# A one-core two-block model: state space layer in plain F32 on VectorE, joined up projections, another place for a weight, and weight splits without GpSimd

## The chip, the cores and the metric

The kernel runs on one core of a Trainium2 chip. The metric is the time of one execution in device microseconds. A core has TensorE (matrix products), VectorE, ScalarE and GpSimd (element by element work), and SyncE, whose queue starts nearly all transfers here. Each engine works through its own instructions in order; engines wait for each other on semaphores. In the profile TensorE is PE (PEld is its weight loading), VectorE DVE, ScalarE ACT, GpSimd POOL and SyncE SP.

## The reference, cut to what matters

The model has 256 tokens, width 1024 and feed-forward width 2816. The first block is a state space layer and stick-breaking attention, each with a feed-forward network behind it whose gate goes through a short convolution; the second has two layers of feed-forward, hybrid mixer, feed-forward. In all there are six networks of the form

```python
def swiglu(x, w13, w2):
    gate, up = jnp.split(x @ w13, 2, axis=-1)
    return (jax.nn.silu(gate) * up) @ w2
```

(two of them with the convolution and other weights). The state space layer is

```python
u = (h @ w_in).reshape(bsz, seq, N_GROUPS, SSM_GROUP)
bu_re = jnp.einsum('blgh,gph->blgp', u, bb_re)
bu_im = jnp.einsum('blgh,gph->blgp', u, bb_im)
_, _, s_re, s_im = lax.associative_scan(combine, (a_seq_re, a_seq_im, bu_re, bu_im), axis=1)
y = jnp.einsum('blgp,ghp->blgh', s_re, c_re) - jnp.einsum('blgp,ghp->blgh', s_im, c_im) + d_skip * u
z = jax.nn.gelu(y.reshape(bsz, seq, D_SSM)) @ w_glu
return z[..., :D_MODEL] * jax.nn.sigmoid(z[..., D_MODEL:])
```

and a mixer ends with `(gate_a * ya + gate_b * yb) @ w_out`, where `ya` and `yb` are two branches behind products of their own.

## The kernel before

**Split products.** Most products are F32 at reduced passes: each operand is split into a high part `h` (a cast) and a low part `l = x - h`, and `mm3` (L179) adds low x high, high x high and high x low in PSUM, three matmuls and three weight loads. `Core.unit` (L158) fetches one weight unit of 128 x 1024 (512 KB) into `raw` (three buffers) on SyncE's queue, casts it on ScalarE into `wh` (L150) and subtracts on VectorE into `wl` (L154). With `share` above zero GpSimd makes that many of the 1024 columns of `wl` in parallel, and VectorE the rest: 512 for units loaded ahead for the next network (`ahead`) and for the mixers' convolutions, 640 for the mixers' z, gate and branch weights and the gate half of `w_glu`, 384 for `w_in`.

**Feed-forward** (`ffn`, L406). The hidden width is 22 columns `m` of 128. Columns 0 and 1 are made ahead of the network by token (`ahead`, `behind`), and the other 20 by `main`: for each of the two halves `c` (gate and up) a chain of eight steps of k, three matmuls of 256 tokens each (`cols_steps`, L199), into one half of a shared PSUM bank. Then `gated`: Silu on ScalarE out of PSUM, the product with the up half on VectorE (L423), and the split into `gh` and `gl`. Seven columns later (`LAG`) the column's down projection follows, twelve matmuls of 512 columns into four accumulating banks; the last six columns are held back and run at the end (`last_rows`). Of eight PSUM banks four accumulate, and at the start two more hold the columns made ahead.

**State space layer** (`ssm`, L501). Z and W hold powers of the decay, built by `step` in growing ranges, Z's on VectorE and W's on GpSimd. `inputs` makes the products with `w_in` (eight units, split as above, against a split input). For each of eight groups kt, `group` makes `gt` from Z and b and `ca` from W and c: a first product on VectorE, a second one (`prod`) on GpSimd, and the addition on VectorE for `gt` and for the first `ca`, on GpSimd for the other seven (`GADD`). Then come the scan and its rotations on VectorE (`t`, `v`, `Sx`), with `turns` (`ea`, `eb`, `er`) four times between. At most three groups are in flight. `weave` fixes TensorE's order by an estimated time, with `inputs` and the first half of the gated output product as filler.

**The output projection of a mixer** (`row_gemm`, L266, with `hold` 5). Units 0 to 2 are used as they come, units 3 to 7 are held, and their products run per output part, over all five each time. Which pool a unit of a stage with `spare` gets is counted by `turn`: every fifth goes to `spare`, the others to the four buffers of `wp`. Held units use the pool `hold` (five buffers, 40,960 bytes a partition) with `hraw` (two raw buffers, 8,192) for their loads; `spare` has 8,192 bytes. The pools lie one on another in the order in which they are opened: `hraw` from 108,768, `hold` from 116,960, `spare` from 157,920 to 166,112. Before, the same bytes belonged to the mixer's own pools, among them `mk2` (123,488 to 150,112), `mk1` (to 164,448) and `keep1` (to 181,856), which holds the gates until the last branch product is gated and split (`gate_b`). Pools are shared out and synchronised by the framework, which also sets the order of instructions on every engine but TensorE.

## Time and profile before

| what | value |
|---|---|
| median of 3 runs | 2254.35 us (2253.45 to 2261.68) |
| the profiled execution | 2259.23 us, of which span 2257.5 us |
| mean granted TensorE clock | 0.976 |
| TensorE busy | 2146.6 us (95%) |
| VectorE busy | 1466.2 us (65%) |
| ScalarE busy | 1102.8 us (49%) |
| GpSimd busy | 510.7 us (23%) |

The profile is that of one execution. Its span is the time between the first and the last instruction. The busy time of an engine is an average over stages; the tables by stretch below are read for a stage. The granted clock is given as a share of full speed.

### The profile page before, as it was taken

The page shows a single profiled execution, that of the slowest core. Times are in us where ns is not written, and L with a number is a line of the kernel's source. Part 1 is how long each engine was busy: PE and PEld are TensorE (multiplying, and loading weights), DVE is VectorE, ACT ScalarE, POOL GpSimd, SP SyncE. Part 2 cuts the span into 40 slices and gives each one's busy share as a digit, 9 for nine tenths or more (in the row PEclk, how much of TensorE's full clock was granted, in tenths as well). Part 3 has the DMA queues.
Part 4 walks back from the last instruction along what each step waited for, and adds up shares of the span by engine and source line. Part 5 has one row for each costly group of instructions (what it writes and reads, how often), then busy time and mean ns, then how long its engine had stood idle before and what let it go on. Part 6 is the DMA issues. An engine that isn't in the chain of part 4 may idle for free.

```text
span 2257.5 us, 40264 instructions
## 1 busy us (share of the span) xinstructions
PE 2146.6 (95%) x15892; PEld 1968.0 (87%) x15892; DVE 1466.2 (65%) x2352; ACT 1102.8 (49%) x1951; POOL 510.7 (23%) x519
## 2 busy tenths in 40 slices
PE   5679999999999999998999899999999899999998
PEld 5568999888999999897889899989989788998997
DVE  8974766676666555689754765565558886466555
ACT  4344554454545544466555444444445656543442
POOL 7542100101000100252534410020015344342000
PEclk8779999999999999999999999999999999999999
DMA  4214576544556556554443655556565454264663
GB/s 153 66 34 149 167 240 188 173 138 140 177 185 197 183 185 187 165 170 145 133 118 121 207 157 186 185 183 197 186 188 157 133 154 122 92 203 154 194 188 121
DMA packets 123486, 362.27 MB, mean 160 GB/s; under 512 B 24732, under 2 KB 38000, under 8 KB 123296
## 3 DMA queue, kind: packets, MB, share of 16 engines
q1 hardware_dynamic: 117696, 350.25, 49.7%
q0 software_dynamic: 5232, 9.37, 1.5%
q8 instruction: 125, 2.05, 0.4%
q14 instruction: 65, 0.53, 0.1%
q10 hardware_dynamic: 368, 0.07, 0.0%
HBM read 355.36 MB, written 5.04 MB: 160 GB/s over the span
## 4 chain that ended last, share of the span: by engine, by line
PE 75%; DVE 10%; DMA 5%; issue 5%; ACT 2%; POOL 1%; ACTq 0%; POOLq 0%; DVEq 0%
PE ps L36 72%; PE ps L40 3%; DVE wl L154 3%; DMA raw<-in_ffn_w_dram 2%; ACT wh L150 2%; DMA raw<-in_w_in_z_dram 1%; DVE xl L154 1%; DMA k<-scratch 1%; DVE keep L1053 1%; DVE k L1053 1%; DVE ea L513 0%; POOL u L1052 0%; DVE keep L1052 0%; DMA raw<-in_w_out_dram 0%; DVE er L709 0%
## 5 line engine op out<-in xcount | busy, mean ns | idle before, releaser
L154 DVE TENSOR_TENSOR wl<-raw,wh 128x1024 fp32r<-128x1024 f32 (+3 forms) x622 | 718.3, 1158 | 543.4 <-ACT wh L150 541.2
L150 ACT CAST wh<-raw 128x1024 fp32r<-128x1024 f32 x622 | 649.4, 1049 | 659.4 <-PE ps L36 344.2
L36 PE MATMUL ps<-xl,wh 128*128 128x256 f32 x3056 | 880.4, 288 | 8.5 <-DVE xl L154 6.2
L36 PE MATMUL ps<-xh,wh 128*128 128x256 f32 x3056 | 866.1, 283 | 0.0
L36 PE MATMUL ps<-xh,wl 128*128 128x256 f32 x3056 | 865.9, 283 | 0.0
L36 PEld LDWEIGHTS ps<-xl,wh 128*128 128x128 f32 x3056 | 587.9, 192 | 32.8 <-issue 19.1
L36 PEld LDWEIGHTS ps<-xh,wh 128*128 128x128 f32 x3056 | 587.2, 192 | 3.9
L36 PEld LDWEIGHTS ps<-xh,wl 128*128 128x128 f32 x3056 | 586.8, 192 | 0.0
L154 POOL TENSOR_TENSOR wl<-raw,wh 128x512 fp32r<-128x512 f32 (+2 forms) x172 | 293.3, 1709 | 1183.9 <-ACT wh L150 1126.7
L36 PE MATMUL ps<-wl,gh 128*128 128x512 f32 x528 | 208.9, 396 | 0.0
L36 PE MATMUL ps<-wh,gl 128*128 128x512 f32 x528 | 208.3, 394 | 0.5 <-DVE gl L154 0.5
L36 PE MATMUL ps<-wh,gh 128*128 128x512 f32 x528 | 208.0, 394 | 0.0
L36 PE MATMUL ps<-wl,xh 128*128 128x256 f32 (+1 forms) x576 | 188.2, 327 | 11.8 <-DVE wl L154 11.8
L36 PE MATMUL ps<-wh,xl 128*128 128x256 f32 (+1 forms) x576 | 183.1, 318 | 0.8 <-DVE xl L154 0.7
L36 PE MATMUL ps<-wh,xh 128*128 128x256 f32 (+1 forms) x576 | 182.4, 317 | 0.0
L36 PEld LDWEIGHTS ps<-wl,xh 128*128 128x128 f32 x576 | 110.7, 192 | 21.4 <-DVE wl L154 12.7
L36 PEld LDWEIGHTS ps<-wh,gl 128*128 128x128 f32 x528 | 99.2, 188 | 24.3 <-DVE gl L154 1.3
L36 PEld LDWEIGHTS ps<-wh,xl 128*128 128x128 f32 x576 | 110.8, 192 | 9.9 <-DVE xl L154 2.7
L36 PEld LDWEIGHTS ps<-wh,xh 128*128 128x128 f32 x576 | 111.0, 193 | 6.5
L36 PEld LDWEIGHTS ps<-wl,gh 128*128 128x128 f32 x528 | 99.7, 189 | 18.8
L36 PEld LDWEIGHTS ps<-wh,gh 128*128 128x128 f32 x528 | 99.2, 188 | 18.5
L150 ACT CAST xh<-ps 128x512 fp32r<-128x512 f32 (+1 forms) x68 | 34.0, 517 | 115.5 <-PE ps L40 113.3
(286 smaller groups left out, 2446.8 us busy)
## 6 DMA issues: line engine op xcount, KB each, us to landing
raw<-in_ffn_w_dram SPq DMA_DIRECT2D x264, 512.0 KB, 4.3
raw<-in_ffn_w_up_dram SPq DMA_DIRECT2D x88, 512.0 KB, 4.1
raw<-in_w_in_qkv_dram SPq DMA_DIRECT2D x48, 512.0 KB, 4.1
raw<-in_ffn_w_down_dram SPq DMA_DIRECT2D x44, 512.0 KB, 3.9
raw<-in_w_in_gate_dram SPq DMA_DIRECT2D x32, 512.0 KB, 3.6
raw<-in_w_branch_dram SPq DMA_DIRECT2D x32, 512.0 KB, 3.6
raw<-in_ssm_w_glu_dram SPq DMA_DIRECT2D x16, 512.0 KB, 3.5
raw<-in_w_in_z_dram SPq DMA_DIRECT2D x16, 512.0 KB, 3.6
```

Source lines behind the costliest of these rows:

```text
L36: self.pe.matmul(out, lhsT=lhsT, rhs=rhs, start=start, stop=stop)
L40: self.pe.transpose(out, in_, ident)
L150: o = [self.nc.scalar.copy(out=h, in_=src).ins]
L154: r = e.tensor_tensor(out=l[..., c], in0=src[..., c], in1=h.bitcast(F32)[..., c], op=ALU.subtract)
L1053: stt = lambda o, a, s, b, op0, op1, e=V: e.scalar_tensor_tensor(out=o, in0=a, scalar=s, in1=b, op0=op0, op1=op1)
```

## The change

(1) In the state space layer the normalised input stays one plain F32 tile, `w_in` is loaded raw and multiplied in plain F32, and all of GpSimd's products and additions go to VectorE. Since the eight `w_in` units no longer pass `unit`, `turn` counts on from another value. (2) In the up projections the high and low parts of the input lie side by side, and a step of k is one matmul of 512 columns (weight high part against both) and one of 256 (weight low part against input high part); each chain takes a PSUM bank of its own, and `fold` adds its two halves (a copy on ScalarE, an addition on VectorE). (3) In the stage of a mixer's output projection `spare` is opened ahead of `hraw` and `hold`, so that it lies from 108,768, `hraw` from 116,960 and `hold` from 125,152 to 166,112. (4) All shares of GpSimd in weight splits go, but for the convolutions'.

```diff
@@ -204,6 +204,28 @@
+    def wide_steps(self, out, w, x):
+        both = out.rearrange("p a b -> p (a b)")
+        for k in range(KD):
+            a = slice(k * P, (k + 1) * P)
+            high = lambda: self.pe.matmul(both, lhsT=w[0][:, a], rhs=x[k][2].rearrange("p a b -> p (a b)"),
+                                          start=k == 0, stop=k == KD - 1)
+            if k < KD - 1:
+                high()
+            self.pe.matmul(out[:, 1], lhsT=w[1][:, a], rhs=x[k][0], start=False, stop=False)
+            if k == KD - 1:
+                high()
+            if k % 3 == 2:
+                yield 1
+    def fold(self, pool, ps):
+        s = pool.tile([P, T], F32, name="sum")
+        self.nc.scalar.copy(out=s, in_=ps[:, 1])
+        self.nc.vector.tensor_tensor(out=s, in0=ps[:, 0], in1=s, op=ALU.add)
+        return s
@@ -228,7 +250,7 @@
             for src in srcs:
-                ws.append([self.unit(src[j], SHARE, stay=True) for j in range(2)])
+                ws.append([self.unit(src[j], stay=True) for j in range(2)])
@@ -314,10 +336,11 @@
-        return tuple(self.hp[i].tile([P, KD, T], F32R, name=f"x{s}") for s in "hl")
+        both = self.hp[i].tile([P, KD, 2, T], F32R, name="xx")
+        return both[:, :, 0], both[:, :, 1], both
     def ktiles(self, x):
-        return [(x[0][:, k, :], x[1][:, k, :]) for k in range(KD)]
+        return [tuple(v[:, k] for v in x) for k in range(KD)]
@@ -381,17 +404,16 @@
-    def silu_gate(self, pool, ps, m):
+    def silu_gate(self, pool, g, m):
         s = pool.tile([P, T], F32, name="s")
-        self.nc.scalar.activation(out=s, in_=ps[:, 0, :], func=AF.Silu)
+        self.nc.scalar.activation(out=s, in_=g, func=AF.Silu)
...
-        def gate(pool, ps, m):
-            g = ps[:, 0, :]
+        def gate(pool, g, m):
@@ -417,10 +439,8 @@
-            def gated(m, ps):
-                s = gate(act, ps, m)
-                p = act.tile([P, T], F32, name="p")
-                nc.vector.tensor_tensor(out=p, in0=s, in1=ps[:, 1, :], op=ALU.mult)
+            def gated(m, s, u, p):
+                nc.vector.tensor_tensor(out=p, in0=s, in1=u, op=ALU.mult)
@@ -440,17 +460,20 @@
                             self.pe.transpose(ps[:, c, t * P:(t + 1) * P], state[c][:, t, m * P:(m + 1) * P], self.ident)
-                    gated(m, ps)
+                    gated(m, gate(act, ps[:, 0, :], m), ps[:, 1, :], act.tile([P, T], F32, name="sum"))
...
                     if m < MF:
-                        ps = self.ps(2, T)
                         for c in range(2):
-                            yield from self.cols_steps(ps[:, c, :], self.unit(up[m - 2, c]), self.ktiles(x))
-                        gated(m, ps)
+                            ps = self.ps(2, T)
+                            yield from self.wide_steps(ps, self.unit(up[m - 2, c]), self.ktiles(x))
+                            if c == 0:
+                                s = gate(act, self.fold(act, ps), m)
+                        u = self.fold(act, ps)
+                        gated(m, s, u, u)
@@ -470,7 +493,6 @@
 LAG = 7
-SHARE = 512
@@ -480,13 +502,8 @@
 HS, HT, GATE, SPACE = 2.7, 5.5, 8, 6.0
-GADD = 1
-WP_ = (1,)
-SH_I = 384
 XO = 1
-SH_Y = 640
 NR = 2
-PT = ()
@@ -601,9 +618,15 @@
                 G.memset(turn[:, 1:], 0.5 * np.pi)
-            hT = c.pair(0)
+            hT = one.tile([P, KD, T], F32, name="hT")
             for t in range(2):
-                c.flip(hT, c.rms(t, c.rms_stat(t), g, c.x[:, t, :]), t)
+                xn = c.rms(t, c.rms_stat(t), g, c.x[:, t, :])
+                for q in range(2):
+                    ps = c.ps(4, P)
+                    for j in range(4):
+                        k = q * 4 + j
+                        PE.transpose(ps[:, j, :], xn[:, k * P:(k + 1) * P], c.ident)
+                    S.copy(out=hT[:, q * 4:q * 4 + 4, t * P:(t + 1) * P], in_=ps)
@@ -666,21 +689,21 @@
-            def step(R, src, dst, n, l, e=V):
+            def step(R, src, dst, n, l):
...
                 ta, tb = (v[:, :, :n] for v in (tmp[:2] if R is Z else tmp[2:]))
-                tt(ta, R[:, :, src], l[:, None, 0:1].to_broadcast(sh_), ALU.mult, e)
-                tt(tb, R[:, ::-1, src], l[:, 1:3, None].to_broadcast(sh_), ALU.mult, e)
-                tt(R[:, :, dst], ta, tb, ALU.add, e)
+                tt(ta, R[:, :, src], l[:, None, 0:1].to_broadcast(sh_), ALU.mult)
+                tt(tb, R[:, ::-1, src], l[:, 1:3, None].to_broadcast(sh_), ALU.mult)
+                tt(R[:, :, dst], ta, tb, ALU.add)
...
             for n, l in ((1, l1), (2, l2), (4, l4)):
-                step(W, slice(0, n), slice(n, 2 * n), n, l, G if WP_[0] else V)
-            step(W, slice(4, 5), slice(8, 9), 1, l4, G if WP_[0] else V)
+                step(W, slice(0, n), slice(n, 2 * n), n, l)
+            step(W, slice(4, 5), slice(8, 9), 1, l4)
@@ -720,13 +743,16 @@
         q1 = c.pool(ctx, "q1", 2)
-        hx = c.ktiles(hT)
         def inputs(kt):
-            w = c.unit(I["ssm_w_in"][kt], SH_I)
+            w = c.raw.tile([P, 1024], F32, name="raw")
+            nc.sync.dma_start(out=w, in_=I["ssm_w_in"][kt])
             pu = c.ps(T)
-            yield from c.cols_steps(pu, w, hx)
+            for k in range(KD):
+                PE.matmul(pu, lhsT=w[:, k * P:(k + 1) * P], rhs=hT[:, k, :], start=k == 0, stop=k == KD - 1)
+                if k % 2:
+                    yield 1
@@ -766,9 +792,8 @@
                 tt(o, f(0), h(x), ALU.mult)
-                tt(p, f(1), h(y), ALU.mult, G)
-                add = (G if R is W and kt >= GADD else V).tensor_tensor(out=o, in0=o, in1=p, op=ALU.add).ins
-                last = last if R is W and kt >= GADD else add
+                tt(p, f(1), h(y), ALU.mult)
+                last = V.tensor_tensor(out=o, in0=o, in1=p, op=ALU.add).ins
@@ -812,7 +837,7 @@
             t1 = q1.tile([P, 8, NC], F32, name="t1")
-            tt(t0, v, Er[:, gs, :], ALU.mult, G if kt in PT else V)
+            tt(t0, v, Er[:, gs, :], ALU.mult)
@@ -821,7 +846,7 @@
             t2, t3 = t0, v
-            tt(t2, sc, Er[:, gs, :], ALU.mult, G if kt in PT else V)
+            tt(t2, sc, Er[:, gs, :], ALU.mult)
...
@@ -1036,10 +1061,7 @@
 LW = 2
-SH_C = (512, 512)
-SH_QA = 0
-SH_G = SH_B = SH_Z = 640
-SH_S = 0
+SH_C = 512
@@ -1122,7 +1144,7 @@
             src = n * NH + m
-            w = c.unit(W("qkv")[src], SH_C[f])
+            w = c.unit(W("qkv")[src], SH_C)
...
@@ -1202,7 +1224,7 @@
             for m in range(KD):
-                w = c.unit(W("gate")[side * KD + m], SH_G)
+                w = c.unit(W("gate")[side * KD + m])
...
@@ -1622,8 +1644,8 @@
             if kind == "mix":
+                c.spare_pool(cn)
                 c.hold_pools(cn, MH, MR)
-                c.spare_pool(cn)
```

## Rows read from the trace of the kernel before

**Rows 1.** Busy time by stretch; columns: stretch, length, then busy us of each engine.

```profile
40.00:105.00 65.00, 38.28 (x262) 31.27 (x262) 64.33 (x49) 24.32 (x46) 44.34 (x18) 0.75 0.30 77
105.00:163.00 58.00, 43.73 (x312) 36.01 (x313) 49.52 (x58) 25.95 (x47) 24.31 (x11) 0.79 0.18 37
163.00:204.00 41.00, 40.99 (x299) 35.26 (x298) 17.58 (x32) 14.41 (x28) 6.46 (x3) 0.94 0.16 32
780.00:840.00 60.00, 60.00 (x449) 57.30 (x448) 32.63 (x40) 27.29 (x39) 0.00 (x0) 1.00 0.62 193
1285.00:1291.00 6.00, 0.02 (x1) 0.02 (x1) 4.44 (x7) 3.34 (x4) 2.08 (x3) 0.71 0.51 137
```

**Rows 2.** VectorE's groups by shape, 0 to 163 us: count, busy us, mean ns.

```profile
L513 DVE TENSOR_TENSOR ca<-W,c_re 128x1152 f32<-128x1152 f32 x7 | 15.6, 2236 | 5.8 <-PE ps L36 5.8
L513 DVE TENSOR_TENSOR gt<-Z,b_re 128x1024 f32<-128x1024 f32 x8 | 13.5, 1702 | 0.0
L513 DVE TENSOR_TENSOR Sx<-t,v 128x248 f32<-128x248 f32 x5 | 10.0, 2009 | 0.0
L770 DVE TENSOR_TENSOR gt<-gt,prod 128x1024 f32<-128x1024 f32 x8 | 9.7, 1212 | 0.1
L709 DVE TENSOR_SCALAR er<-er 128x512 f32<-128x512 f32 x4 | 9.4, 2358 | 0.0
L154 DVE TENSOR_TENSOR wl<-raw,wh 128x640 fp32r<-128x640 f32 x8 | 8.7, 1092 | 0.0
L513 DVE TENSOR_TENSOR eb<-count,turnl 128x512 f32<-128x512 f32 x4 | 8.5, 2115 | 0.0
...
L513 DVE TENSOR_TENSOR ea<-count,turnh 128x512 f32<-128x512 f32 x4 | 6.3, 1585 | 0.2 <-ACT Er L717 0.2
L521 DVE TENSOR_SCALAR sm<-sm 128x64 f32<-128x64 f32 x11 | 5.6, 641 | 0.0
L513 DVE TENSOR_TENSOR ea<-ea,er 128x512 f32<-128x512 f32 x4 | 5.0, 1258 | 0.1
...
L513 DVE TENSOR_TENSOR ea<-ea,eb 128x512 f32<-128x512 f32 x4 | 2.7, 680 | 0.0
```

**Rows 3.** GpSimd's groups by shape, whole span.

```profile
L513 POOL TENSOR_TENSOR prod<-W,c_im 128x1152 f32<-128x1152 f32 x8 | 20.6, 2572 | 7.2 <-DVE gt L770 7.0
L770 POOL TENSOR_TENSOR ca<-ca,prod 128x1152 f32<-128x1152 f32 x7 | 19.9, 2848 | 27.0 <-DVE ca L513 27.0
```

**Rows 4.** Timeline of TensorE in a steady feed-forward stretch: start, us.

```profile
862.32 0.28 PE L36 MATMUL ps<-xl,wh 128*128 128x256 f32 x1
...
868.07 0.40 PE L36 MATMUL ps<-wl,gh 128*128 128x512 f32 x1
...
870.87 0.28 PE L36 MATMUL ps<-xl,wh 128*128 128x256 f32 x1
```

**Rows 5.** Timeline of TensorE around 1020 us: four plain F32 records.

```profile
1020.06 1.02 PE L36 MATMUL ps<-keep 128*128 128x256 f32 x4
1020.92 0.38 PE L40 MATMUL ps<-ident,k 128*128 128x128 f32 x2
```

**Rows 6.** VectorE's groups by shape, whole span.

```profile
L154 DVE TENSOR_TENSOR wl<-raw,wh 128x1024 fp32r<-128x1024 f32 x450 | 551.6, 1229 | 457.4 <-ACT wh L150 456.4
L154 DVE TENSOR_TENSOR wl<-raw,wh 128x384 fp32r<-128x384 f32 x80 | 79.8, 997 | 45.6 <-ACT wh L150 45.4
...
L423 DVE TENSOR_TENSOR p<-s,ps 128x256 f32<-128x256 f32 x132 | 54.7, 414 | 1.8 <-ACT s L386 0.9 <-ACT s L401 0.8
```

**Rows 7.** Chain of waits, 1283 to 1300 us: start, us, what.

```profile
1281.59 3.73 DMA raw<-in_ffn_w_dram
...
1287.11 1.50 DVE xl L154
...
1288.62 1.05 ACT wh L150
...
1290.98 9.13 PE ps L36 x32
```

More of the change, by code (lines that the diff above doesn't have):

```diff
@@ L934, in keys @@
         def keys(m):
-            w = c.unit(I["kv_w_k"][m], SH_S)
+            w = c.unit(I["kv_w_k"][m])
             pk = c.ps(T)
@@ L949, in query @@
         def query(m):
-            w = c.unit(I["attn_w_q"][m], SH_S)
+            w = c.unit(I["attn_w_q"][m])
             pq = c.ps(T)
@@ L1164, in plain @@
         def plain(src, dst, scale):
-            w = c.unit(src, SH_QA)
+            w = c.unit(src)
             p = c.ps(T)
@@ L1174, in qkv_a @@
             p = c.ps(2, T)
-            yield from c.toks256_steps(p, W("va")[0], hT, SH_QA)
+            yield from c.toks256_steps(p, W("va")[0], hT)
             ka["v"] = keep2(2, T)
@@ L1189, in z_gate @@
             p = c.ps(2, T)
-            yield from c.toks256_steps(p, W("z")[n], hT, SH_Z)
+            yield from c.toks256_steps(p, W("z")[n], hT)
             z_done(n, p)
@@ L1212, in branch @@
             for m in range(KD):
-                w = c.unit(I["w_branch_2"][side, i, m], SH_B)
+                w = c.unit(I["w_branch_2"][side, i, m])
                 p = c.ps(T)
```

2 lines of the change are left out of this document (1 added, 1 removed).

## The prediction

> **What bounds the kernel now.** I read the table of busy time by stretch first, because the share over the whole span (TensorE 95%) hides that one stage is bound by another engine. In the steady feed-forward stretch TensorE is busy for 60.00 of 60 us at granted clock 1.00, and VectorE for about half of it; in the state space layer from 40 to 105 us it is VectorE that is busy for 64.33 of 65 us, with TensorE at 38.28 us and granted clock 0.75, and GpSimd at 44.34 us [rows 1]. From 105 to 163 us neither is full (VectorE 49.52, TensorE 43.73 of 58), and from 163 to 204 us TensorE is, 40.99 of 41 [rows 1]. So VectorE's time counts up to about 163 us, and from there on TensorE's pace, except at a few places. Then I read VectorE's forms up to 163 us against the same shape elsewhere [rows 2], GpSimd's forms [rows 3], TensorE's pace from start to start (ends are modelled, so I use distances of starts) [rows 4, 5], the weight splits [rows 6], and the chain of waits where TensorE stands still before an output projection [rows 7].
>
> **State space layer.** The change does three things here. (a) GpSimd's arithmetic goes to VectorE. What VectorE pays: second products 8 x 1.212 (1024 wide) and 8 x 1.364 (1152 wide, 1.212 x 9/8), seven additions of 1152 at 1.364, together 30.2 us; and twelve operations on W, for which no free row of the shape stands here: between 0.25 us each (a 64-column operation can't be dearer than the 0.414 of 256 columns) and 0.68 (512 wide), 3 to 8 us; most are 256 wide or less, so I take 5. Sum +35.2 us [rows 2, 6]. What it gets back: the same forms are stretched now, in the stretch in which GpSimd works. Against the free price of their width: gt 8 x (1.702 - 1.212) = 3.9; ca 7 x (2.236 - 1.364) = 6.1; Sx 5 x (2.009 - 0.414) = 8.0; er 4 x (2.358 - 0.680) = 6.7; eb 4 x (2.115 - 0.680) = 5.7; ea 4 x (1.585 - 0.680) = 3.6 and 4 x (1.258 - 0.680) = 2.3; the 64-column operations at least 11 x (0.641 - 0.414) = 2.5. Sum -38.8 [rows 2, 6]. GpSimd's own pieces last as long as these stretches (2.57 and 2.85 us) [rows 3]. (b) w_in is no longer split, nor the layer's input: 8 x 1.092 = 8.7 and four halves of 0.68 = 2.7 go, -11.4 [rows 2]. Net of (a) and (b): 35.2 - 38.8 - 11.4 = -15.0 us of VectorE. In addition a product of 1152 that took 2.57 us on GpSimd, and its addition that took 2.85, take 1.36 each [rows 3]; a group's next step waits for them, 2.7 us a group. With eight groups, three of them in flight together, I count a quarter of that, 5 us. That gives -20. Lower bound of the gain: 3, if VectorE's stretched time was waiting that comes back as waiting for TensorE between 105 and 163 us, where it has room of 8.5 us already. Upper bound: 38, all of the stretched time, if what I priced as moved falls into gaps.
>
> The Trainium skill (SBUF — State Buffer, "SBUF: two separate sides") says that VectorE and GpSimd share one pair of ports, held for a whole instruction, and that the loser is blocked until it ends. Taken at its word all of the 38.8 us goes with GpSimd's work, as I count; the rows agree in size, a stretched Sx of 2.01 beside GpSimd's pieces of 2 to 3 us.
>
> (c) The eight input products become plain F32. Two records of one such product with 256 columns stand 0.86 us per four records, 0.43 per product [rows 5], where the three split ones are 0.36 [rows 4]: 64 x (0.43 - 0.36) = +4.5 us of TensorE work. Up to 105 us TensorE is idle for more than 26 us [rows 1], so I cost it at nothing; if that cover is gone it costs the 4.5. The Trainium skill (FP8 and Floating Point Precision, "TensorE Precision Notes") gives true FP32 four passes, against three reduced ones here; by that alone it would be four thirds of 0.36, 0.48, and +7.7 us; the row is lower and decides. Without the splits the first product also starts earlier; that lies within the range.
>
> **Up projections.** 6 networks x 20 columns m x 2 x 8 = 1920 steps of k. A step is three matmuls of 256 columns now: 48 of them lie between 862.32 and 868.07, 0.120 each, 0.360 a step [rows 4]. It becomes one of 512 columns and one of 256: twelve of 512 take 868.07 to 870.87, 0.233 each [rows 4], so 0.353. The 512 columns were measured with weight rows as moving operand, and next to each other; nothing here shows the two sizes in turn. Bounds: 0.347 (the saved weight load takes another 6 ns with it) to 0.362 (the change of size costs what is saved). I take 0.354, 6 ns x 1920 = -11 us; range -25 to +4. Added is the fold: per chain a copy of 256 columns on ScalarE and an addition of 256 on VectorE, 0.41 us each (the price of p, which also reads PSUM) [rows 6]. Per column m of 8.5 us that is 0.82 on each; VectorE is busy for 32.63 and ScalarE for 27.29 of 60 us [rows 1], so it fits: nothing, for as long as it runs beside the next chain. A column uses two PSUM banks instead of one, and four are free beside the accumulators, so two columns, 17 us, are in flight. At the start of a network two of the four still hold the state: +1 us over the six networks, between 0 and 6.
>
> **Weight place.** In the two output projections after the mixers TensorE stops; in the first it is busy for 0.02 of the 6.00 us from 1285 to 1291 [rows 1]. The second mixer has the same code. The chain runs: a feed-forward weight lands (1281.59 + 3.73), is cast and split, the last gate split ends (1287.11 + 1.50), then the cast and the split of the third output weight, then TensorE [rows 7]. That weight lies in `spare`, which overlaps the mixer's pool `keep1`, and its cast waits for the last user of that pool though the tile itself does not touch it. With the order of the pools turned, `spare` lies at the lowest address, where the mixer is done early; `hold` (five units) now reaches 1,664 bytes into `keep1`. So I expect these 6 us to go and the five held units to wait for the same split instead: late next is the fifth. With R the end of that split: two are cast and split at R + 2.3 and R + 3.5, as their raw tiles are free early; `hraw` has two buffers, so the next two come a load (3.7), a cast (1.05) and a split (1.23) later, at about R + 8.5 and R + 9.7, and the fifth at R + 14.6. The last loop needs it after 4 x 0.69 us and has 3 x 3.4 + 0.7 us of products left, so the end is R + 25.6. Before, the end was 1310.0. Behind these loads on SP's queue stand the next network's four first weights; they are needed only at that end. R is the open number: 1288.6 as now gives +4.2, 1286 (the split next to GpSimd takes 1.50, free 0.41, and its wl before it is no longer halved) +1.6, and 1281, right behind the last branch product, -3.4. I take +2 for each mixer, +4. If the wait is only for the tiles that overlap, four units are ready early, and the gain is 6 to 8 each, -14. Range -16 to +14.
>
> **GpSimd's split shares.** 80 splits go from 0.997 on VectorE, for 384 of 1024 columns, to 1.229 for all of them [rows 6], and 36 of half width I price the same: 116 x 0.232 = 27 us more of VectorE work, and GpSimd's part of each goes. VectorE has room there (32.63 of 60 us in the steady stretch [rows 1]), so nothing, but at the ends of networks the splits of the weights loaded ahead stand before the normalisation on VectorE: +0.5 us at some six of them, +2 net of the lock that goes; range -3 to +4.
>
> **Sum.** -20 - 11 + 1 + 4 + 2 = -24 us. The profiled execution took 2259.23 us, 4.9 above the median of the runs (2254.35), so 2235 in its own terms, and **2230 us** in terms of the median.
>
> **Rivals.** *The state space layer is TensorE's after all.* For it: from 163 us on TensorE is full, and at 105 to 163 us it has 43.73 of 58 at clock 0.79 [rows 1]. Then VectorE's 15 us come back as waiting, the 4.5 us of F32 count, and only 8 net are gained there: 2242 us. *The pair of sizes is no faster.* Then the up projections give 0 to +4 instead of -11: 2242 us. *More comes than I count.* The output projections lose their stop without a new one (-14 in place of +4) or the whole stretched time goes (-32 in place of -20): 2200 to 2216 us. *Slower: the fold stops the chain.* ScalarE works in order. If its queue holds the fold of a chain ahead of the cast of the next chain's weight, the cast waits for the chain's end, and TensorE for 0.41 (copy) + 0.4 (Silu) + 1.05 (cast) + 1.23 (split) = 3.1 us. Between the two chains of a column no product of the down projection lies, so nothing covers it; 120 such places make up to 370 us, and from 8 of them on the gain is gone; at one in six the time is 2292 us. Against it: the steady stretch has no gap in TensorE [rows 1] though Silu stands at the same place, so casts run at least one unit ahead.
>
> **Chances.** Forecast 0.54 (its own range 2214 to 2246); layer bound by TensorE 0.13; no faster pair 0.10; more than counted 0.14; slower by the fold 0.09. A measurement of this kernel tells 0.5%, 11.3 us, from no change. Faster by more than that, below 2243: nearly all of the forecast, half of the next two, all of the fourth, 0.77. Within: 0.14. Slower: 0.09. Range: 2202 to 2250; the slower rival and the far end of the fourth lie outside.
>
> **What would show it.** Right: VectorE's Sx, er and eb near their free price, the end of the layer near 183 us instead of 203; in the steady stretch a step near 0.354 and no gap in TensorE; at the output projections no stop after the second unit but one before the last held unit, with casts of held units right behind the last gate split. Wrong: TensorE waiting for ScalarE or VectorE within up chains, a step of 0.36 or more, or a VectorE that stays full up to 160 us.

## The result, and the profile after

The changed kernel takes 2224.90 us (median of 4 runs, 2223.28 to 2227.32) against 2256.64 us of the kernel before beside it: a ratio of 0.9858, 95% interval 0.9835 to 0.9882, or 31.7 us less. The profiled execution has a span of 2221.5 us, 36.0 less than that of before; of the difference to 31.7, some 4 us is the spread of single executions (2259.23 us is 2.6 above the median of before, 2223.28 is 1.6 below that of after).

The starts of a few products of TensorE, read from the timelines of the two profiled executions, split the 36 us by stage:

| TensorE has come to | before, us | after, us | gained in the stage |
|---|---|---|---|
| first down product of network 1 (state space layer, gated output) | 290.13 | 266.96 | 23.2 |
| last down product of network 3 (networks 1 to 3, attention) | 944.47 | 919.21 | 2.1 |
| last branch product, first mixer | 1279.00 | 1248.54 | 5.2 |
| first product behind its output projection | 1310.02 | 1282.12 | -2.6 |
| last down product of network 5 | 1692.66 | 1660.66 | 4.1 |
| last branch product, second mixer | 2027.81 | 1991.56 | 4.3 |
| first product behind its output projection | 2059.43 | 2025.63 | -2.5 |
| last down product of network 6 | 2248.13 | 2212.18 | 2.1 |

One profile is not sharper than this: four profiles of kernels with the same code up to the first row have it between 261.6 and 267.0 us, and the two with the code of before at 285.88 and 290.13, so differences of a few us in that stage are not read from it: its gain lies between 19 and 29 us.

Busy time by stretch of the changed kernel; columns as in [rows 1]: the stretch, its length, busy us (and instructions) of TensorE, its weight loading, VectorE, ScalarE and GpSimd, then the granted clock, the DMA share and GB/s.

```profile
40.00:105.00 65.00, 56.21 (x379) 47.52 (x377) 54.92 (x77) 35.75 (x60) 0.00 (x0) 0.87 0.38 96
105.00:163.00 58.00, 50.12 (x340) 41.95 (x341) 36.24 (x59) 27.19 (x50) 0.00 (x0) 0.85 0.22 39
...
780.00:840.00 60.00, 60.00 (x317) 51.09 (x316) 37.33 (x51) 31.96 (x50) 0.00 (x0) 1.00 0.60 186
```

Against [rows 1]: from 40 to 105 us GpSimd is at 0, VectorE at 54.92 us instead of 64.33, and TensorE is busy for 56.21 us instead of 38.28, at clock 0.87 instead of 0.75. In the steady stretch TensorE is still full, with 317 matmuls instead of 449. VectorE's groups by shape, 0 to 163 us (count, busy us, mean ns):

```profile
L530 DVE TENSOR_TENSOR prod<-W,c_im 128x1152 f32<-128x1152 f32 x8 | 10.8, 1349 | 0.0
...
L530 DVE TENSOR_TENSOR ca<-W,c_re 128x1152 f32<-128x1152 f32 x8 | 10.7, 1348 | 6.0 <-PE ps L36 6.0
...
L530 DVE TENSOR_TENSOR Sx<-t,v 128x248 f32<-128x248 f32 x7 | 2.9, 408 | 0.0
...
L530 DVE TENSOR_TENSOR eb<-count,turnl 128x512 f32<-128x512 f32 x4 | 2.7, 682 | 0.0
```

The stretched forms of [rows 2] are at the free price at which I had set them: Sx 0.408 instead of 2.009, eb 0.682 instead of 2.115, ca 1.348 instead of 2.236; the product that took 2.57 us on GpSimd [rows 3] takes 1.35. Only er, a scalar operation, came lower than set: 0.416, not 0.680. The layer's last output product starts at 182.2 us instead of 198.2. TensorE in the steady stretch, timeline (start, us):

```profile
780.73 0.27 PE L36 MATMUL ps<-xx,wl 128*128 128x256 f32 x1
...
781.08 0.28 PE L36 MATMUL ps<-xx,wl 128*128 128x256 f32 x1
...
782.81 0.28 PE L36 MATMUL ps<-xx,wl 128*128 128x256 f32 x1
```

The smaller matmul is shown; six steps from 780.73 to 782.81 make 0.347 each, and the mean over 755 to 905 us is 0.350 (0.117 and 0.233). Before, a step was 0.360 [rows 4], and 0.357 on the mean. Last, the chain of waits in the first mixer's output projection (start, us, what); [rows 7] answers to it.

```profile
1252.02 0.35 DVE xx L154
...
1252.39 1.06 ACT wh L150
...
1253.47 1.24 DVE wl L154
1254.72 5.78 DMA raw<-in_w_out_dram
...
1260.53 1.05 ACT wh L150
...
1261.60 1.24 DVE wl L154
1262.86 3.45 DMA raw<-in_w_out_dram
...
1266.33 1.05 ACT wh L150
1267.40 1.24 DVE wl L154
...
1268.69 10.63 PE ps L36 x39
```

The last gate split ends at 1252.37, and at 1252.39 ScalarE casts held units. The third waits for a load (5.78 us) behind the split of the first, the last for another (3.45), and TensorE goes on at 1268.69. The stop ahead of unit 2 in [rows 7] is gone; two others have come, of 4.8 us behind 1258.06 and of 3.5 us behind 1265.19.

### The profile page after: what moved, and what is told of

It reads as the page before. It is cut to its first block, busy times and chain, and to the rows that moved or that the text cites. A ratio compares the mean times of both kernels' runs of the same rounds, so it can differ in the third digit from the quotient of the medians.

```text
span 2221.5 us, 36550 instructions
## 1 busy us (share of the span) xinstructions
PE 2135.0 (96%) x13908; PEld 1867.4 (84%) x13908; DVE 1537.0 (69%) x2615; ACT 1182.5 (53%) x2187; POOL 226.9 (10%) x360
## 4 chain that ended last, share of the span: by engine, by line
PE 74%; DVE 8%; DMA 7%; issue 4%; ACT 3%; POOL 1%; POOLq 0%; SPq 0%; DVEq 0%; ACTq 0%
PE ps L36 71%; PE ps L40 3%; DVE wl L154 3%; ACT wh L150 2%; DMA raw<-in_w_out_dram 2%; DMA raw<-in_ffn_w_dram 1%; DMA raw<-in_ffn_w_down_dram 1%; DMA raw<-in_w_in_z_dram 1%; DMA raw<-in_ssm_w_glu_dram 1%; DVE keep L1075 1%; DMA k<-scratch 1%; DVE prod L530 1%; POOL k L1074 0%; DVE k L1075 0%; DMA raw<-in_kv_w_v_dram 0%
## 5 line engine op out<-in xcount | busy, mean ns | idle before, releaser
L36 PE MATMUL ps<-xx,wh 128*128 128x256 f32 (+1 forms) x4064 | 1077.4, 340 | 4.6 <-DVE xx L154 2.6
L154 DVE TENSOR_TENSOR wl<-raw,wh 128x1024 fp32r<-128x1024 f32 (+1 forms) x614 | 738.1, 1204 | 332.5 <-ACT wh L150 322.7
L36 PE MATMUL ps<-xx,wl 128*128 128x256 f32 x2992 | 803.4, 282 | 0.6 <-DVE wl L154 0.6
L36 PEld LDWEIGHTS ps<-xx,wh 128*128 128x128 f32 x4064 | 686.4, 191 | 91.9 <-issue 18.9
L36 PEld LDWEIGHTS ps<-xx,wl 128*128 128x128 f32 x2992 | 568.4, 190 | 22.0 <-DVE wl L154 0.8
L36 PE MATMUL ps<-wh,xx 128*128 128x256 f32 (+1 forms) x1152 | 258.3, 318 | 0.8 <-DVE xx L154 0.7
L36 PE MATMUL ps<-wl,xx 128*128 128x256 f32 (+1 forms) x576 | 189.7, 329 | 19.3 <-DVE wl L154 18.7
L36 PEld LDWEIGHTS ps<-wh,xx 128*128 128x128 f32 x1152 | 193.5, 193 | 16.5 <-DVE xx L154 3.0
L226 DVE TENSOR_TENSOR sum<-ps,sum 128x256 f32<-128x256 f32 x240 | 101.2, 423 | 112.1 <-ACT sum L225 112.1
L36 PEld LDWEIGHTS ps<-wl,xx 128*128 128x128 f32 x576 | 111.0, 193 | 31.9 <-DVE wl L154 22.6
```

What stands on the lines that cost most here:

```text
L36: self.pe.matmul(out, lhsT=lhsT, rhs=rhs, start=start, stop=stop)
L154: r = e.tensor_tensor(out=l[..., c], in0=src[..., c], in1=h.bitcast(F32)[..., c], op=ALU.subtract)
L226: self.nc.vector.tensor_tensor(out=s, in0=ps[:, 0], in1=s, op=ALU.add)
```

## The experiments

Each kernel is timed beside the kernel before; the ratio to it stands with its 95% interval (0.9858, 0.9835 to 0.9882, for the changed one). Differences are those of the medians (2224.90 us for the changed kernel); taken through the ratios they come out within 1.8 us of these. Where the intervals of two kernels overlap, their difference is not clear of noise, and the text says so.

**GpSimd's arithmetic back in the state space layer.** Theory: VectorE's operations stand while GpSimd works. Rival: the gain came from the input product.

```diff
-                step(W, slice(0, n), slice(n, 2 * n), n, l)
+                step(W, slice(0, n), slice(n, 2 * n), n, l, G)
...
-                tt(p, f(1), h(y), ALU.mult)
-                last = V.tensor_tensor(out=o, in0=o, in1=p, op=ALU.add).ins
+                tt(p, f(1), h(y), ALU.mult, G)
+                add = (G if R is W and kt >= 1 else V).tensor_tensor(out=o, in0=o, in1=p, op=ALU.add).ins
+                last = last if R is W and kt >= 1 else add
```

> The changed kernel with GpSimd's arithmetic of the state space layer back on GpSimd (the steps of W, the second products, seven additions); the plain F32 input product stays. Theory (VectorE's operations stand still while GpSimd works, and VectorE sets the pace up to 163 us): Sx, er, eb and ca are stretched again (Sx near 2 us instead of 0.41), and the layer with its gated output ends 12 to 22 us later than in the changed kernel, 2237 to 2247 us. Rival (most of the 23 us came from the input products without splits): less than 8 us slower, under 2233 us.

Measured: 2259.44 us, ratio 1.0015 (1.0004 to 1.0027): 34.5 us slower than the changed kernel, and no faster than the kernel before. Theory and rival both set it too low; the rival falls. Its profile, busy time by stretch, then VectorE's forms to 163 us, then timelines of GpSimd and VectorE (start, us, in brackets the idle time before and who ended it):

```profile
40.00:105.00 65.00, 43.16 (x242) 35.12 (x242) 50.26 (x50) 23.32 (x43) 24.95 (x10) 0.71 0.25 62
105.00:163.00 58.00, 38.20 (x254) 32.60 (x253) 40.34 (x41) 22.55 (x41) 19.62 (x8) 0.76 0.26 71
```

```profile
L530 DVE TENSOR_TENSOR ca<-W,c_re 128x1152 f32<-128x1152 f32 x6 | 14.3, 2402 | 9.7 <-PE ps L36 9.7
...
L530 DVE TENSOR_TENSOR eb<-count,turnl 128x512 f32<-128x512 f32 x4 | 8.5, 2114 | 0.0
...
L530 DVE TENSOR_TENSOR Sx<-t,v 128x248 f32<-128x248 f32 x4 | 3.5, 869 | 0.1
```

```profile
83.35 2.37 POOL L530 TENSOR_TENSOR prod<-W,c_im 128x1152 f32<-128x1152 f32 x1 [4.17 <-DVE gt L796]
102.57 3.53 POOL L796 TENSOR_TENSOR ca<-ca,prod 128x1152 f32<-128x1152 f32 x1 [16.86 <-DVE ca L530]
106.18 2.89 POOL L530 TENSOR_TENSOR prod<-Z,b_im 128x1024 f32<-128x1024 f32 x1
```

```profile
92.39 0.43 DVE L530 TENSOR_TENSOR t<-t,Er 128x256 f32<-128x256 f32 x1
101.13 1.36 DVE L530 TENSOR_TENSOR ca<-W,c_re 128x1152 f32<-128x1152 f32 x1 [8.32 <-PE ps L36]
```

The forms are stretched again (eb 2.11, ca 2.40, Sx 0.87). But VectorE is busy for only 50.26 of 65 us here, less than in the changed kernel, and the first down product starts 34.6 us later all the same, at 301.51 us. So VectorE's busy time is not the whole price. GpSimd finishes a product at 85.7 and then stands for 16.86 us until 102.57, since its next piece, an addition, needs `ca` from VectorE, and VectorE makes that `ca` only at 101.13, 8.32 us idle, when TensorE has let its buffer go. The product of the next group stands behind the addition in GpSimd's queue and starts at 106.18. The three engines wait for each other in turn, and with one engine fewer in the round each turn is shorter. That is read from these rows; no run tests it by itself.

The 34.5 us are the price in this kernel, with the plain F32 input. In the kernel before, with the same arithmetic on GpSimd and split inputs, the first down product starts 11 to 16 us earlier than here (285.88 and 290.13 us in two profiles). The two kernels differ there in the plain input, the shares, the joined chains and the counter of turns; which of them costs this beside GpSimd was not separated. With split inputs the same stage goes from 286 to 290 us with GpSimd's arithmetic to 257 to 263 without it (three profiles), 23 to 33 us, the shares in it taken out too.

**Split inputs instead of plain F32.** The input and `w_in` are split again, on ScalarE and VectorE alone; the counter of turns moves back with it.

```diff
-            w = c.raw.tile([P, 1024], F32, name="raw")
-            nc.sync.dma_start(out=w, in_=I["ssm_w_in"][kt])
+            w = c.unit(I["ssm_w_in"][kt])
             pu = c.ps(T)
-            for k in range(KD):
-                PE.matmul(pu, lhsT=w[:, k * P:(k + 1) * P], rhs=hT[:, k, :], start=k == 0, stop=k == KD - 1)
-                if k % 2:
-                    yield 1
+            yield from c.cols_steps(pu, w, hx)
```

> The changed kernel with the layer's input and w_in split into high and low parts again, on VectorE and ScalarE alone (no GpSimd), three matmuls a step; GpSimd's arithmetic stays on VectorE, and the counter of turns moves back by eight units, so that in the output projections unit 2 holds spare as before the change. Theory: VectorE gets 8 x 1.23 + 4 x 0.68 = 12.5 us more ahead of its work, TensorE 4.5 us less; up to 60 us VectorE is the later one, so 4 to 12 us slower, 2229 to 2237 us. Rival (plain F32 costs TensorE what the splits cost VectorE): within 3 us of 2225.

Measured: 2222.74 us, 0.9845 (0.9826 to 0.9864): 2.2 us faster, which is not clear of noise: as the rival has it, not 4 to 12 slower. But two things differ, so the counter was moved alone.

**The counter of turns alone.**

```diff
-        self.early, self.norm, self.spare, self.turn = None, [], None, 0
+        self.early, self.norm, self.spare, self.turn = None, [], None, 3
```

> The changed kernel with nothing changed but the counter of turns, which starts at 3, so that the same units go to spare as before the change (in the output projections of the mixers unit 2, in the state space layer's gated output those of before); the input product stays plain F32. The kernel with split inputs (2222.7 us) began the first down projection of the first network 10 us earlier than the changed kernel and lost 6 of them again further on, and both the plain product and the counter differ in it. If the plain F32 product is what costs the 10 us, this kernel keeps that cost and takes over the later losses: 2225 to 2232 us, first down projection near 267 us. If the counter is what costs them (a stop of 3.8 us for a weight of the gated output stands at 203 us in the changed kernel and not there), it begins near 257 us and the time is 2218 to 2223 us.

Measured: 2229.35 us, 0.9878 (0.9861 to 0.9895): 4.5 us slower than the changed kernel, with intervals that overlap, and the first down product at 265.1 us. So the first expectation holds, and the counter is not what cost the 10 us. That the counter costs the 4.5 us is not shown. The two output projections do last 36.3 and 35.9 us instead of 33.6 and 34.1, 4.5 us together; but in four kernels with the counter and the pools of the changed one (chains undone, GpSimd's arithmetic back, shares back, fold doubled) they last 34.2 to 36.9 us too. There the load behind the first held split varies: 7.63 us with the chains undone and 7.10 with the fold doubled, in the first mixer, against 5.78. And the profile with the moved counter has a first mixer that is 5.7 us longer and three networks and an attention that are 4.2 us shorter than the changed kernel's.

With the counter the same, splitting the inputs gives 2222.74 against 2229.35: the plain F32 product costs some 6.6 us. Two later pairs with four held units, told below, give 8.1 (2204.12 against 2196.04, the counter moved) and 3.8 us (against 2200.35, the counter the same), so 4 to 8 us; by the intervals each of the three is known to some 5 to 7 us only, but they have one sign. The plain products among TensorE's groups to 204 us, in the kernel with counter 3:

```profile
L36 PE MATMUL ps<-hT,raw 128*128 128x256 f32 x128 | 31.6, 398 | 0.0
```

Their records take 31.6 us. Over all profiles with the arithmetic on VectorE the layer's last output product starts at 177 to 182 us with plain inputs (eight kernels) and at 166 to 171 with split ones (three), 11 us earlier on the mean. Of this lead 7 us are lost again: from there to the first down product it takes 83 to 85 us with plain inputs and 91 with split ones. The rest is of the size of the 4 to 8 us. No mechanism is shown for either part.

**The joined chains of the up projections undone.**

```diff
-                        for c in range(2):
-                            ps = self.ps(2, T)
-                            yield from self.wide_steps(ps, self.unit(up[m - 2, c]), self.ktiles(x))
...
+                        ps = self.ps(2, T)
+                        for c in range(2):
+                            yield from self.cols_steps(ps[:, c, :], self.unit(up[m - 2, c]), self.ktiles(x))
+                        gated(m, gate(act, ps[:, 0, :], m), ps[:, 1, :], act.tile([P, T], F32, name="sum"))
```

> The changed kernel with the up projections' chains as before: three matmuls of 256 columns a step of k into half of a shared bank, no fold (the input stays side by side in one tile). Theory: the joined step saves TensorE 6.7 ns (0.350 instead of 0.357 in the steady stretch of the two profiles) in 1920 steps, 13 us, and the fold is hidden: 9 to 14 us slower than the changed kernel, 2234 to 2239 us. Rival (the fold or the second PSUM bank costs something at the ends of networks that the steady stretch does not show): less than 6 us slower, under 2231 us.

Measured: 2233.44 us, 0.9897 (0.9881 to 0.9913), 8.5 us slower; between the two expectations and next to the theory's, since the two intervals leave it open by about 6 us. From the first product behind the second output projection to the last down product, the last network takes 188.71 us against 186.55: 2.16 us, which would make 13 for six. Of the 11.5 us between the two profiles 4.7 lie in the output projections (36.6 and 35.8 us instead of 33.6 and 34.1), which the edit does not touch. So the step is worth 8 to 13 us, by an estimate from these two numbers.

**The fold doubled.** The copy twice, and one more operation on VectorE, in each of 240 chains.

```diff
         self.nc.scalar.copy(out=s, in_=ps[:, 1])
+        self.nc.scalar.copy(out=s, in_=ps[:, 1])
         self.nc.vector.tensor_tensor(out=s, in0=ps[:, 0], in1=s, op=ALU.add)
+        self.nc.vector.tensor_tensor(out=s, in0=s, in1=s, op=ALU.max)
```

> The changed kernel with the fold's work doubled: the copy on ScalarE is made twice and VectorE makes one more operation of 256 columns behind the addition, in each of the 240 chains (0.37 us and 0.41 us more). Theory (both lie beside TensorE's products, with room for them): no more than 2 us slower, 2223 to 2227 us. Rival (fold on the path, now and then or always): a tenth of 240 x 0.8 is 19 us; 5 us or more slower, 2230 us or more.

Measured: 2227.67 us, 0.9870 (0.9850 to 0.9890): 2.8 us, neither expectation, and not to be told from none by the intervals. The busy time in the steady stretch:

```profile
780.00:840.00 60.00, 60.00 (x318) 51.09 (x317) 42.78 (x66) 35.96 (x65) 0.00 (x0) 1.00 0.57 186
```

VectorE rises from 37.33 to 42.78 us and ScalarE from 31.96 to 35.96, and TensorE stays full. The last network, with 40 of the 240 doubled folds, takes 139.09 us from its first to its last down product, 139.08 in the changed kernel. So of 187 us of added work none shows there, and in the total no more than the noise lets through, some 10 us.

**The order of the two pools, in both kernels.** First the changed kernel with the old order, then the kernel before with the new order and nothing else.

```diff
                 c.spare_pool(cn)
                 c.hold_pools(cn, MH, MR)
-                c.spare_pool(cn)
```

(the second; the first is its reverse.)

> The changed kernel (2224.9 us) with the two pools of a mixer's output projection opened in the old order again; all else as changed. In the changed kernel the stage from the last branch product to the first product of the next network lasts 33.6 us in the first mixer and 34.1 in the second (31.0 and 31.6 before the change). My theory, that a pool which overlaps the mixer's gate pool waits as a whole for the last gate split, says: now only spare waits, and since the counter of turns has moved it holds unit 0 instead of unit 2, so TensorE stops once, for some 6 us, ahead of unit 0, and then runs through eight units without a stop: 6 + 8 x 2.8 + 1.5 = 30 us, 3 to 4 us less than changed for each mixer, 2217 to 2219 us in all. Rival (the new place is what helps, and what costs 2.5 us a mixer lies elsewhere): the stage gets longer than 34 us, 2227 us or more.

Measured: 2230.80 us, 0.9880 (0.9862 to 0.9897), 5.9 us slower, with intervals that overlap: against the theory's number, and in the rival's range. The stage lasts 33.8 and 35.5 us, 0.2 and 1.4 more than changed; the other 7 us of the profile lie in the second mixer ahead of that stage and were not pursued (on VectorE the framework ordered some weight splits otherwise there). The stop ahead of unit 0 is there, as the theory says, but lasts 9 us, not 6:

```profile
1251.29 1.23 DVE wl L154
...
1253.32 0.44 DVE xx L154
1253.78 1.05 ACT wh L150
...
1256.14 5.88 PE ps L36 x17
```

The gate split ends only at 1253.76, later than I took it, behind a weight of the next network. From the first product there is no further stop.

> The kernel before, with nothing changed but the order of these two pools. The whole-pool wait says: the stop ahead of unit 2 goes, and stops ahead of the last held units come, the last of them ready at R + 14.6 to 16.3 with R about 1288; the stage lasts 33 to 36 us instead of 31: 2 to 5 us more for each mixer, 2260 to 2267 us. Rival (the place alone removes the stop): 24 to 26 us a stage, 2242 us.

Measured: 2268.59 us, 1.0052 (1.0039 to 1.0066), 12 us slower than the kernel before, a little over the upper end of the theory's range; the rival falls. The stage lasts 37.5 and 36.9 us instead of 31.0 and 31.6. The chain of waits shows the same sequence as in the changed kernel: gate split, cast, split, a load of 5.83 us, and another of 3.60 before TensorE goes on.

```profile
1283.07 1.45 DVE xl L154
...
1284.54 1.06 ACT wh L150
...
1286.88 5.83 DMA raw<-in_w_out_dram
...
1295.06 3.60 DMA raw<-in_w_out_dram
...
1301.04 2.07 PE ps L36 x4
```

So by itself the new place costs 12 us in the kernel before; in the changed kernel, with the counter moved, it costs nothing that the stage would show. With the old order the counter decides which unit waits: the stop is ahead of unit 2 and 6.6 us long in the kernel before, and ahead of unit 0 and 9 us long in the changed one.

**Four held units instead of five.** Then the pool of held units ends below the gate pool.

```diff
-MH, MR = 5, 2
+MH, MR = 4, 2
```

> The changed kernel with four held units instead of five in the mixers' output projections (MH 4), so that the hold pool ends at 157,920 and no longer reaches into the gate pool; unit 3 goes through the ordinary buffers. By the theory of the whole-pool wait the stops of 4.4 and 2.9 us ahead of the last held units go, and the stage lasts about 8 x 2.8 + 2 = 24 to 27 us: 7 to 10 us less for each mixer, 2205 to 2211 us. Rival (the held units wait for their loads and the two raw buffers, not for the gate pool): the stage stays above 31 us, 2220 us or more.

Measured: 2204.12 us, 0.9765 (0.9750 to 0.9780), 20.8 us faster than the changed kernel. The stages last 22.9 and 22.8 us. Busy time of the two stages, of this kernel and then of the changed one:

```profile
1244.10:1267.00 22.90, 22.90 (x108) 18.83 (x106) 16.38 (x25) 6.56 (x8) 1.69 (x2) 1.00 0.62 207
1981.50:2004.20 22.70, 22.70 (x106) 18.71 (x105) 14.51 (x21) 6.19 (x7) 1.69 (x2) 1.00 0.56 186
```

```profile
1248.60:1282.10 33.50, 26.20 (x106) 20.40 (x106) 19.72 (x26) 10.07 (x12) 1.69 (x2) 0.85 0.50 187
1991.60:2025.60 34.00, 26.37 (x107) 20.49 (x106) 19.45 (x25) 9.85 (x12) 1.69 (x2) 0.90 0.55 183
```

TensorE is full, 22.90 of 22.90 us at clock 1.00, against 26.20 of 33.50 at 0.85. The two raw buffers are still two. And the eight loads of the output weight are all issued by 1241.03 us, before the last gate split ends at 1250.00; in the changed kernel the last three are issued from 1254.72 on, behind that split (1252.37). So the loads were late because the held casts waited for the gate pool. (One held unit fewer would also shorten the row of loads behind such a wait; here there is no wait left for it to follow.)

**GpSimd's shares back** in the units loaded ahead and in the mixers' z, gate and branch weights.

```diff
-                w = c.unit(W("gate")[side * KD + m])
+                w = c.unit(W("gate")[side * KD + m], 640)
...
-                ws.append([self.unit(src[j], stay=True) for j in range(2)])
+                ws.append([self.unit(src[j], 512, stay=True) for j in range(2)])
```

> The changed kernel with GpSimd's shares back in the units loaded ahead (512 columns) and in the mixers' z, gate and branch weights (640); the state space layer, up projections and pools as changed. My prediction had +2 us for taking them out, so by it this kernel is about 2 us faster, 2223. Against it stands the trace: between the last down product of a network and the last branch products of the mixer behind it the changed kernel is 4.8 us shorter in the first mixer and 3.8 in the second; if that is the shares, this kernel is 6 to 10 us slower, 2231 to 2235 us.

Measured: 2236.21 us, 0.9912 (0.9893 to 0.9930), 11.3 us slower. From the last down product before a mixer to the first product of its last branch it takes 315.8 and 314.1 us, 307.7 and 309.2 in the changed kernel; the output projections take 36.2 and 36.4 instead of 33.6 and 34.1. The profiled execution is the slowest of six (2243.33 us), so by stage the loss looks larger than it is. Two stretches of the first mixer, of this kernel and of the changed one:

```profile
976.00:1076.00 100.00, 88.70 (x627) 78.20 (x627) 83.71 (x184) 59.12 (x123) 40.50 (x55) 0.95 0.46 143
1076.00:1180.00 104.00, 102.03 (x986) 92.45 (x985) 68.39 (x196) 58.96 (x187) 43.59 (x62) 0.98 0.36 109
```

```profile
975.00:1075.00 100.00, 91.44 (x661) 81.42 (x660) 84.45 (x193) 62.30 (x133) 38.88 (x54) 0.97 0.48 148
1075.00:1170.00 95.00, 95.00 (x946) 85.56 (x944) 60.63 (x187) 55.27 (x175) 19.11 (x46) 1.00 0.38 113
```

The first stretch of 100 us holds 627 matmuls with the shares and 661 without, at clock 0.95 and 0.97; the second has 986 in 104 us against 946 in 95. Over both, with 1613 and 1607 matmuls, VectorE is busy for 152.1 us with the shares and for 145.1 without, in 204 and 195 us, though with them it has fewer columns to split. Over the whole first mixer, up to its last branch, it is even, in 315.8 and 307.7 us:

```profile
920.90:1236.70 315.80, 302.52 (x2563) 276.46 (x2562) 220.61 (x503) 177.66 (x425) 140.59 (x162) 0.98 0.43 136
```

```profile
919.20:1226.90 307.70, 299.12 (x2563) 273.68 (x2562) 221.35 (x503) 177.49 (x425) 88.12 (x131) 0.99 0.45 139
```

The splits of weights take VectorE 68.1 us of it with the shares and 77.4 without, and everything else 152.5 against 144.0: what it saves in columns it loses in longer operations beside GpSimd (a form of 128 x 256, `keep` from `k`, sixteen times, takes 0.759 us on the mean instead of 0.689). TensorE has the same 2563 matmuls and is busy 3.4 us longer, at clock 0.98 instead of 0.99, and idle 4.7 us longer. Which wait makes the mixer longer was not found, nor which of the two sets of weights does it.

**The last share out too** (the convolutions'), on top of four held units: `SH_C` 0 for 512.

> Four held units, and the last share of GpSimd, that in the 48 convolution weights, taken out too; else as the changed kernel (2204.1 us with four held units alone). VectorE gets 48 x 0.29 = 14 us more and GpSimd 77 us less. If the shares cost what they cost elsewhere in the mixers (4 to 5 us a mixer for some 40 units), 2194 to 2200 us. If VectorE, which is busier in the stretch of the convolutions, becomes the late one there, 2206 to 2216 us.

Measured: 2215.64 us, 0.9821 (0.9803 to 0.9838): 11.5 us slower than with four held units alone. The first expectation falls, the second holds. The first mixer takes 320.2 us up to its last branch against 307.2, so there the share pays. Which stage of it loses shows in its busy time against that of the kernel with four held units alone, from the start of the mixer:

```profile
914.90:974.00 59.10, 57.66 (x447) 52.99 (x446) 45.38 (x75) 34.93 (x57) 5.81 (x11) 1.00 0.52 158
974.00:1074.00 100.00, 88.11 (x606) 77.69 (x605) 77.33 (x175) 55.71 (x117) 23.91 (x44) 0.93 0.45 132
```

```profile
914.80:974.00 59.20, 59.18 (x461) 54.73 (x460) 49.38 (x82) 35.80 (x59) 29.42 (x26) 1.00 0.48 151
974.00:1074.00 100.00, 91.79 (x667) 81.83 (x665) 84.55 (x195) 61.83 (x135) 36.51 (x53) 0.97 0.48 152
```

TensorE falls from 59.18 to 57.66 and from 91.79 to 88.11 us, at clock 0.93 instead of 0.97 in the second. Its waits for VectorE in the mixer come to 10.4 us against 2.2 with four held units alone; the two longest (us in total, times, longest us):

```profile
PE ps L36 <- DVE keep L1075: 4.0, 1, 4.0
PE ps L36 <- DVE wl L154: 2.6, 1, 2.6
```

So VectorE is the late one there.

**Four held units and split inputs together.**

> Four held units (2204.1 us alone) and split inputs (2222.7 alone, 2.2 under the changed kernel) together. With four held units the output projections of the mixers have no stop whichever unit goes to spare, so what the split inputs lost there does not come back: 10 us less than four held units alone, 2193 to 2200 us. If the gain of the split inputs is only a shift between stages, 2201 to 2206 us.

Measured: 2196.04 us, 0.9735 (0.9716 to 0.9753): 60 us under the kernel before and 29 under the changed one, the fastest of all; the first expectation holds. With the counter as in the changed kernel besides (`turn` from 2):

> Four held units and split inputs (2196.0 us) with the counter of turns started at 2, so that the units that go to spare are those of the changed kernel. In the changed kernel moving the counter back cost 4.5 us, as much as the two output projections got longer (36.3 and 35.9 us instead of 33.6 and 34.1). If that is the only way in which the counter acts, it does nothing here, where these stages have no stop: 2193 to 2199 us. If it also acts elsewhere, 2189 to 2192 us.

Measured: 2200.35 us, 0.9746 (0.9720 to 0.9771). The median is 1.4 over the first expectation, and the intervals cover each other: no effect of the counter is to be seen where the output projections have no stop.

## Why the prediction was right, and where not

I had forecast 2230 us, 24 less; it came to 2224.90, 31.7 less. The total held, within its range. By stage of the two profiles three of the four terms came near their numbers and the fourth, the shares, missed by 11 us; but within two of the three, errors of opposite sign cancel, and that is luck.

**State space layer.** "That gives -20" came to 23.2 us in the profile (19 to 29 with the other profiles of the same code), inside the bounds of 3 and 38, but its parts are not mine. The arithmetic alone stood in the sum at -8.6 (35.2 - 38.8 - 5); taking it from GpSimd is worth 34.5 us in the kernel with plain inputs (2259.44 against 2224.90). I summed VectorE's busy time and counted "a quarter" of the shorter products as 5 us; what is left out there is, by the rows above, GpSimd's own queue, in which the next group's product stands behind an addition that waits for VectorE and TensorE. The splits stood at -11.4 and the plain F32 product was "cost at nothing", for TensorE's idle 26 us; together they gain nothing: splitting again is 4 to 8 us faster (2229.35 against 2222.74, 2204.12 against 2200.35 and 2196.04). The idle time of [rows 1] is not there after the change: with the arithmetic on VectorE TensorE is busy for 56.21 of 65 us. The price for that case, 4.5, was set, but I did not take it. So -20 held because one part gave far more than I summed and the other nothing. The row of 0.43 us for a plain product holds (16 records from 27.68 to 31.1 us, 0.43 a pair), below the 0.48 that I had worked out from the Trainium skill (FP8 and Floating Point Precision, "TensorE Precision Notes"); the row decides. The Trainium skill's rule on the shared ports (SBUF — State Buffer, "SBUF: two separate sides") agrees with the stretched forms, which came back to 0.41, 0.68 and 1.35 us when GpSimd was taken out; that rule prices one operation, not the queue behind it.

**Up projections.** -11 us and +1 for the fold's banks: the run with the chains undone gives 8.5, six times the last network 13. The 512-column matmul keeps its 0.233 beside one of 256, and the smaller one came down to 0.117; 0.354 was taken, 0.347 to 0.350 is there. The fold costs nothing that the runs can tell; the slower rival did not come.

**Weight place.** "+2 for each mixer" came to +2.6 and +2.5, by the mechanism described: no stop behind unit 2, held casts right behind the last gate split, TensorE on at 1268.69 with the fifth held unit. The stop of 4.8 us ahead of the third held unit was not forecast. The number held by luck. +2 stands for a last gate split that ends 7.4 us behind the start of the last branch product; it ended 3.8 us behind it (1252.37 against 1248.54), and took 0.35 us in the chain instead of the 1.50 of [rows 7]. From there to the end of the stage I had 25.6 us, and it took 29.8: the fifth held unit was ready after 16.3 us, not 14.6 (a load took 5.78 us, not 3.7), and the products behind it took 13.4, not 11.0, at a granted clock of 0.89 behind the two stops. Four held units show that the wait is for the pool. The same place costs 12 us in the kernel before, where the last gate split ends 6.3 us behind the last branch product; how much of the difference is the counter of turns is not shown.

**GpSimd's split shares.** "+2 net" was wrong in size and sign: taking them out gives 11.3 us by the runs, and the mixers are 5.2 and 4.3 us shorter in the two profiles. I priced 27 us of added work on an engine with room and set the lock's end against it with no number. In the first mixer the splits do take VectorE 9.3 us more without the shares, but its other operations take 8.5 less. The mean of 0.997 for the part of 384 columns [rows 6] hid it: those are splits only, and say nothing of the mixer's other operations beside GpSimd. That makes VectorE's time even; what makes the mixer shorter on top stays open. The sign is not general: in the convolutions the same edit costs 11.5 us.

**The sum.** Set against the table by stage, -20 came to -23.2, -10 to -8.3 (networks and attention), +4 to +5.1 and +2 to -9.5 (the mixers): -35.9 in the profiles, where nearly all of the 12 us beyond the forecast are the shares. Undone one at a time the parts do not add up: 34.5 + 11.3 + 8.5 us are 54; less the 4 to 8 us that the plain product loses this is still more than the 31.7 measured. The 34.5 were taken beside a plain input, and with split inputs the same stage gains 23 to 33; and the order of the pools alone has either sign. So the 31.7 can't be handed out in shares from these runs. One bound of the prediction is added up wrongly: of "more comes than I count" the second case alone (-32 in place of -20) gives 2218 us, not 2216.

## What to carry to other kernels

Where VectorE and GpSimd work on one chain, compare each form's mean with the same shape when the other engine is silent, and look at the queue behind the slow engine too: moving the arithmetic gave 34.5 us where the sum over stretched and moved operations had 8.6. Idle time counts as cover only as it stands after the change, not before it. A pool that reaches into an older one by a few bytes can wait for the older one as a whole; one held buffer fewer, which ends the overlap, gave 20.8 us where turning the order had given nothing. A stage whose stops hang on loads varies by itself, here by 3 us between kernels with the same code in it; check that before a difference of that size is put down to an edit.

## What the runs showed of the hardware that I had not expected

One engine's share of a split can have either sign within one mixer: 640 columns of the z, gate and branch weights, with 512 of the weights loaded ahead, cost 11.3 us on GpSimd, while 512 columns of the convolutions' weights there gave 11.5. And VectorE's operations of one input were stretched beside GpSimd as well as those of two (er, a scalar operation, 2.36 us [rows 2], 0.42 in the changed kernel).
